# A two-layer attention and GLA trunk on one core: three stretches of instruction order rewritten

## The chip, the core and the metric

The kernel runs on one core of one Trainium2 chip. The core has engines with a queue each, and each queue is worked off in order: PE (TensorE) multiplies matrices, DVE (VectorE) and ACT (ScalarE) do elementwise work, POOL (GpSimd) does almost nothing here, and SP (SyncE) issues nearly all DMA transfers. Engines wait for one another through semaphores alone, so an instruction that waits holds up whatever stands behind it on its own engine. The metric is the time of one execution in microseconds (us), as the median of the runs.

## The reference

A decoder trunk of two layers over 1024 tokens of width 1024, in float32. Layer 0 mixes tokens with dilated sliding-window attention in three head groups, layer 1 with gated linear attention (GLA); each mixer is followed by a squared-ReLU MLP of width 4096.

```python
def reference(x, ...):
    for i in range(DEPTH):
        h = rmsnorm(x, norm_mix_w[i])
        if i % N_MIXERS == 0:
            x = x + dilated_attention(h, attn_w_in[j], attn_w_out[j])
        else:
            x = x + gla_mixer(h, gla_w_in[j], gla_w_gate_up[j], gla_b_gate[j], gla_norm_w[j], gla_w_out[j])
        h = rmsnorm(x, norm_mlp_w[i])
        x = x + sq_relu_mlp(h, mlp_w_up[i], mlp_w_down[i])
    return rmsnorm(x, final_norm_w)

def rmsnorm(x, w):
    return x * rsqrt(mean(x * x, axis=-1) + 1e-5) * w
```

What the change touches are three products with a norm beside them: the values of the attention, `h @ w_in` for three groups of 1024 columns; the values and the output gate of GLA, two further such products, of which the gate goes through silu; and the second half of the last MLP's `@ w_down` with the final `rmsnorm`.

## The kernel before

**Arithmetic.** Every matmul operand is cut into a rounded part (`hi`, fp32r) and the rest (`lo`): ACT copies the operand to fp32r, DVE subtracts that copy. One product then takes three matmuls, hi x hi, hi x lo and lo x hi (L213 to L215, L829, L1581). Large products are done by a seven-product scheme on 2x2 halves: the left operand's halves are `a11`, `a12`, `a21`, `a22` and four sums `s1` to `s4`, and seven products go into two accumulators, A and B, of four PSUM banks each, one bank for each block of 128 rows. There are eight banks in all.

**Values (L745 to L876).** `Values` computes one 1024x1024 product for each of three groups g. A group has 14 steps n = 14g + 2q + m: q is the product (operands in the order `ORDER`, L497: a12, a11, s1, s2, s4, s3, a22), m a half of the inner dimension. Each step has its weights loaded (`load`, SP), combined with those kept (`total`, DVE), rounded (`rounded`, ACT), their rest taken (`remain`, DVE; `prep` is the last three together), and multiplied (`product`, 24 matmuls of 128x512, six for each of four row blocks t). `sums` takes finished blocks out of PSUM: `copy` on ACT, `add` on DVE, then a store. Steps q = 0 go to B, q = 1 to A; their sum is the output block `c11`.

**The start (L1268 to L1373).** The first 1024 rows, x, come as four tiles of two row blocks. `Halves.norm` (L318, through L243 to L252) takes the squares of a pair on ACT, the inverse root over small ops on DVE and ACT, and scales with the norm weight `wbc` on DVE; `turn` transposes a pair on PE, four 128x128 into a bank, and ACT copies the bank out; `cut` makes hi and lo of 512 columns. Here the order of the work is written out by hand: pair 0, then steps 0 to 2 for row blocks 0 and 1, then pair 1, step 3, pair 2, and so on; `product(4)` (the first with `s1`) follows when all four pairs are turned. From step 8 a loop runs `sums`, `prep(n + 2)`, `load(n + 5)`, `product(n)`.

**GLA's values and gate (L878 to L929, L1729 to L1797).** `Mixed` is the same with 28 steps: g = 0 is the gate, g = 1 the values. The gate's blocks are kept in tiles `gq` of four blocks each from the pool `h8` (12 slots); silu is worked off one block for each step: `begin` (exp, ACT), `guard` (DVE), `logs` (two ACT passes), `close` (three DVE passes and a store to `ggscr`). In the loop over n, `W.pump()` (L161) issues the loads of the next weights and puts their rounding on ACT and DVE; it is called from n = 24 on. The pool `k4` (25 slots of 4 KB a partition) holds weights, their hi and lo, the sums' hi and lo, and the pair tiles; `t2` (8 slots) the small blocks.

**The end (L1646 to L1650, L1672 to L1703).** The last product ends in `run_end`: for each of the last four row blocks, 12 matmuls, `add` into x, then `half_out` (square on ACT, times the norm weight on DVE). After every second block the inverse root of both is taken in one chain (`rstd_of`, L225) and four halves are scaled and stored by SP, 256 KB each.

Of the kernel before, what the change touches and what calls it, by code (L numbers as in the profile page):

```python
# [41 lines left out]
def hybrid_trunk(ctx, tc, x, norm_mix, norm_mlp, norm_fin, a_in, a_out, g_in, g_up, g_b, g_nw,  # L42
# [702 lines left out]
    class Values:  # L745

        STEPS = 14 * NG
        small = False
        BLOCKS = ((1, 0), (0, 0), (0, 1), (1, 1), (1, 1), None, (1, 0))

# [100 lines left out]
        def sums(self, n):  # L851

            g, q, m = self.place(n)
            if q == 0 and g and m == 0:
                for t in range(4):
                    self.add("c21", "B", t, g - 1)
            for t in (2 * m, 2 * m + 1):
                if q == 1:
                    self.copy("c11", "B", t, g)
# [18 lines left out]
    class Mixed(Values):  # L878

        STEPS = 28  # L880
        small = True

        def __init__(self):
            super().__init__()
            self.quad, self.todo, self.open, self.last = {}, deque(), None, None

# [3 lines left out]
        def copy(self, name, s, t, g):  # L890
            if g:
                return super().copy(name, s, t, g)
            if t == 0:
                self.quad[name] = h8([P, 4, 512], F32, "gq")
            c = self.c[name, t] = self.quad[name][:, t, :]
            act.activation(c, self.acc[s][t], AF.Copy)
# [6 lines left out]

        def begin(self):

            if self.todo:
                d = t2([P, 512], F32, "gd")
                act.activation(d, self.todo[0][0], AF.Exp, scale=-1.0)
                self.open = [*self.todo.popleft(), d]

        def guard(self):
            if self.open is not None:
                dve.tensor_scalar(self.open[3], self.open[3], 1.0, 3e38, op0=OP.add, op1=OP.min)

        def logs(self):
            if self.open is not None:
                e = t2([P, 512], F32, "ge")
                act.activation(e, self.open[3], AF.Ln)
                act.activation(e, e, AF.Exp, scale=-1.0)
                self.last, self.open = [*self.open, e], None  # L920

        def close(self):
            if self.last is not None:
                c, rows, cols, d, e = self.last
# [3 lines left out]
                sp.dma_start(ggscr[rows, cols], c)  # L928
                self.last = None  # L929

# [336 lines left out]

    x0 = []  # L1268
    vals = Values()
    for p in range(NB // 2):  # L1270
        t = h8([P, 2, D], F32, "x0")
        for i in range(2):
            sp.dma_start(t[:, i, :], x[0, 256 * p + 128 * i:256 * p + 128 * i + 128, :])
        x0.append(t)
        if p == 0:
            wbc = load_norm_w(norm_mix[0])
            sp.dma_start(ident, ident_d)
            for n in range(4):
                vals.load(n)
    sp.dma_start(masks, msk)  # L1280
    hs = Halves(x0, wbc, vals, None)
    hs.norm(0, (512, 768, 0, 256), 256)
    vals.rounded(0)
    hs.turn(0, (2, 3))
    vals.remain(0)
    hs.cut("a12", 0)
    hs.turn(0, (0, 1))
    vals.prep(1)
    hs.cut("a11", 0)
    vals.prep(2)  # L1290
    vals.prep(3)
    hs.norm(1)
    for n in range(3):
        vals.product(n, [0, 1])
    hs.norm(2)
    hs.turn(1)
    vals.product(3, [0, 1])
    hs.cut("a12", 1)
    hs.cut("a11", 1)
    vals.load(4)  # L1300
    vals.load(5)
    hs.turn(2)
    hs.sum1(0)
    vals.total(4)
    hs.rstd(3)
    hs.norm(3)
    for n in range(2):
        vals.product(n, [2, 3])
    hs.cut("s1", 0)
    vals.rounded(4)  # L1310
    hs.turn(3)
    vals.remain(4)
    vals.product(2, [2, 3])
    vals.total(5)
    vals.sums(2)
    hs.sum1(1)
    hs.cut("s1", 1)
    vals.sums(3)
    vals.rounded(5)
    vals.product(3, [2, 3])  # L1320
    vals.remain(5)
# [7 lines left out]
    hs.cut("s2", 1)  # L1329
    vals.sums(4)  # L1330
    vals.sums(5)
    vals.remain(6)
# [5 lines left out]
    for c in range(2):  # L1338
        hs.cut("s4", c)
    hs.sum3()  # L1340
    vals.load(9)
    for n in range(6, 8):
        vals.sums(n)
        vals.load(n + 4)
        vals.product(n)
        vals.prep(n + 2)
        if n == 6:
            for c in range(2):
                hs.cut("s3", c)
        else:  # L1350
            for c in range(2):
                hs.cut("a22", c)
    vals.load(12)
    for n in range(8, vals.STEPS):
        if n == 12:
# [9 lines left out]
        if n == vals.STEPS - 1:  # L1365
            heads.stage(0, 2)
            heads.stage(0, 3)
        vals.sums(n)
        vals.prep(n + 2)
        vals.load(n + 5)  # L1370
        vals.product(n)
# [136 lines left out]
    class Down:  # L1508
# [117 lines left out]
        def hook(self, n):  # L1626
# [19 lines left out]
            elif n >= 52:  # L1646
                ss = sm([P, 2, 2], "ss")
                for t in (2 * (n - 52), 2 * (n - 52) + 1):
                    self.fin[t] = (ss, k4([P, D], F32, "fin"))
                    self.half_out(t, 1)  # L1650

# [19 lines left out]

        def half_out(self, t, n):  # L1672
            ss, o = self.fin[t]
            sl = slice(512 * n, 512 * n + 512)
            r = self.rows(4 + t)[:, sl]
            junk = t2([P, 512], F32, "junk")
            act.activation(junk, r, AF.Square, accum_out=ss[:, t % 2, n:n + 1])
            dve.tensor_tensor(o[:, sl], r, self.wbc[:, sl], op=OP.mult)

        def run_end(self):  # L1680

            for t in range(4):
                self.product(54, [t])
                self.product(55, [t])
                self.add("B", 1, t, 0)
                if self.spill is not None:
                    self.between(t)
                    continue
                self.half_out(t, 0)
                if t % 2 == 0:  # L1690
                    continue
                ss, _ = self.fin[t]
                v = sm([P, 2], "v")
                dve.tensor_tensor(v, ss[:, :, 0], ss[:, :, 1], op=OP.add)
                y = rstd_of(v, 2, 1.0 / D)
                for u in (t - 1, t):
                    _, o = self.fin.pop(u)
                    dst = out[0, 512 + 128 * u:640 + 128 * u, :]
                    k = u % 2
                    act.activation(o[:, :512], o[:, :512], AF.Copy, scale=y[:, k:k + 1])  # L1700
                    sp.dma_start(dst[:, :512], o[:, :512])
                    dve.tensor_scalar(o[:, 512:], o[:, 512:], y[:, k:k + 1], None, op0=OP.mult)
                    sp.dma_start(dst[:, 512:], o[:, 512:])  # L1703

# [24 lines left out]
    def gla_values():  # L1729
# [9 lines left out]
        m.load(5)  # L1739
        hs.sum1(0)  # L1740
        hs.cut("s1", 0)
        m.sums(2)
        m.product(2)
        m.prep(4)
        hs.sum1(1)
        hs.cut("s1", 1)
        m.load(6)
        m.sums(3)
        m.product(3)
        m.prep(5)  # L1750
        for c in range(2):
            hs.sum2(c)
        hs.cut("s2", 0)
        m.load(7)
        m.total(6)
        for n in range(4, m.STEPS):
            if n != 13:
                m.guard()
                m.close()
            if n != 5:  # L1760
                m.sums(n)
            if n == 4:
                m.sums(5)
                hs.cut("s2", 1)
            m.prep(n + 2)
            m.load(n + (4 if n < 5 else 5))
# [309 lines left out]
```

## Time and profile before

| what | us |
|---|---|
| median of 3 runs | 2612.7 (2612.32 to 2613.21) |
| the profiled execution, its time | 2613.06 |
| its span, first to last instruction | 2611.3 |
| ACT busy | 1276.7 (49%) |
| DVE busy | 1858.9 (71%) |
| PE weight loads (PEld) busy | 2157.3 (83%) |

The span lies inside the execution's own time; 1.8 us are around it. A busy PE isn't a PE at its peak: matmuls overlap, so one is shown with about 0.39 us although the next starts 0.23 us later. Lost PE time is therefore read from start times and counts. In rows of the timeline the first two numbers are start and length in us, xN is a count of merged instructions, and brackets give the engine's idle time ahead of the row and what ended it. Lnnn is a line of the kernel, SPq the queue that issues DMAs. On a row of groups, the numbers behind the bar are busy us in all and mean ns of one.

### The profile page before, as it was taken

The page shows a single profiled execution, that of the slowest core. Times are in us where ns is not written, and L with a number is a line of the kernel's source. Part 1 is how long each engine was busy: PE and PEld are TensorE (multiplying, and loading weights), DVE is VectorE, ACT ScalarE, POOL GpSimd, SP SyncE. Part 2 cuts the span into 40 slices and gives each one's busy share as a digit, 9 for nine tenths or more (in the row PEclk, how much of TensorE's full clock was granted, in tenths as well). Part 3 has the DMA queues.
Part 4 walks back from the last instruction along what each step waited for, and adds up shares of the span by engine and source line. Part 5 has one row for each costly group of instructions (what it writes and reads, how often), then busy time and mean ns, then how long its engine had stood idle before and what let it go on. Part 6 is the DMA issues. An engine that isn't in the chain of part 4 may idle for free.

```text
span 2611.3 us, 33042 instructions
## 1 busy us (share of the span) xinstructions
PE 2586.3 (99%) x12144; PEld 2157.3 (83%) x12144; DVE 1858.9 (71%) x2986; ACT 1276.7 (49%) x2319; POOL 1.8 (0%) x7
## 2 busy tenths in 40 slices
PE   8999999999999999999999999999999999999998
PEld 6888888888888888888888887878888888888887
DVE  7645888888888768666657577977658866666566
ACT  6332455555556446555533345654326545553343
POOL 0000000000000000000000000000000000000000
PEclk9999999999999999999999999999999999999999
DMA  5533465655556733454775452463513544396543
GB/s 190 169 129 124 103 161 131 163 147 150 155 151 183 227 121 128 167 169 137 283 252 185 137 194 93 133 199 97 187 66 123 170 153 157 131 355 200 189 146 125
DMA packets 327010, 423.12 MB, mean 162 GB/s; under 512 B 19808, under 2 KB 192224, under 8 KB 326848
## 3 DMA queue, kind: packets, MB, share of 16 engines
q1 hardware_dynamic: 326848, 421.01, 51.0%
q8 instruction: 95, 1.56, 0.3%
q14 instruction: 67, 0.55, 0.1%
HBM read 279.71 MB, written 116.06 MB: 152 GB/s over the span
## 4 chain that ended last, share of the span: by engine, by line
PE 87%; DVE 8%; ACT 3%; issue 1%; DMA 1%; SPq 0%; ACTq 0%; DVEq 0%
PE pX L598 16%; PE pB L1581 13%; PE pV L598 11%; PE pA L1581 10%; PE pY L598 5%; PE pZ L598 5%; PE pB L829 5%; PE pd L215 3%; PE pd L213 3%; PE pd L214 3%; PE pA L829 3%; PE pO L1017 2%; PE pS L976 2%; PE pP L1003 1%; DVE dl L814 1%
## 5 line engine op out<-in xcount | busy, mean ns | idle before, releaser
L1581 PE MATMUL pB<-dh 128*128 128x512 f32 x512 | 199.4, 389 | 0.0
L1581 PE MATMUL pB<-dh,dl 128*128 128x512 f32 x512 | 199.2, 389 | 0.0
L1581 PE MATMUL pB<-dl,dh 128*128 128x512 f32 x512 | 199.2, 389 | 0.0
L222 DVE TENSOR_TENSOR dl<-sin,dh 128x1024 fp32r<-128x1024 f32 x112 | 136.5, 1218 | 44.6 <-ACT dh L219 44.2
L219 ACT ACTIVATE dh<-sin 128x1024 fp32r<-128x1024 f32 x112 | 117.8, 1052 | 89.7 <-PE pB L1581 32.5
L219 ACT ACTIVATE dh<-kept 128x1024 fp32r<-128x1024 f32 x64 | 67.9, 1061 | 183.4 <-DVE kept L1546 137.8
L598 PE MATMUL pV<-s4h,wd 128*128 128x512 f32 x448 | 150.8, 398 | 0.0
L1581 PE MATMUL pA<-dh,dl 128*128 128x512 f32 x384 | 149.4, 389 | 0.0
L1581 PE MATMUL pA<-dl,dh 128*128 128x512 f32 x384 | 149.4, 389 | 0.0
L1581 PE MATMUL pA<-dh 128*128 128x512 f32 x384 | 149.4, 389 | 0.0
L992 ACT ACTIVATE pt<-pt,orow 128x128 f32<-128x128 f32 (+1 forms) x192 | 84.8, 443 | 96.7 <-DVE orow L990 94.6
L1581 PEld LDWEIGHTS pB<-dh,dl 128*128 128x128 f32 x512 | 96.1, 188 | 20.1
L1581 PEld LDWEIGHTS pB<-dh 128*128 128x128 f32 x512 | 96.1, 188 | 19.9
L1581 PEld LDWEIGHTS pB<-dl,dh 128*128 128x128 f32 x512 | 96.1, 188 | 19.8
L536 DVE TENSOR_TENSOR wal<-raw,wah 128x512 fp32r<-128x512 f32 x112 | 76.2, 686 | 42.9 <-ACT wah L535 42.9
L607 ACT ACTIVATE c<-c 128x512 f32<-128x512 f32 x64 | 40.4, 632 | 122.6 <-DVE c L635 78.9
L598 PEld LDWEIGHTS pV<-s4h,wd 128*128 128x128 f32 x448 | 84.2, 188 | 17.7 <-DVE rb L623 0.2
L222 DVE TENSOR_TENSOR dl<-kept,dh 128x1024 fp32r<-128x1024 f32 x64 | 78.3, 1224 | 25.1 <-ACT dh L219 19.3
L536 DVE TENSOR_TENSOR wbl<-t,wbh 128x1024 fp32r<-128x1024 f32 x56 | 68.6, 1225 | 38.3 <-ACT wbh L535 38.3
L990 DVE CUSTOM_DVE_ANT_0 pt<-pS,masks 128x128 f32<-128x128 f32 (+1 forms) x192 | 58.2, 347 | 51.2 <-PE pS L976 51.2
L598 PE MATMUL pY<-a12h,wah 128*128 128x512 f32 x224 | 89.5, 400 | 0.0
L598 PE MATMUL pZ<-a22h,wgh 128*128 128x512 f32 x224 | 89.3, 399 | 0.0
(336 smaller groups left out, 7364.2 us busy)
## 6 DMA issues: line engine op xcount, KB each, us to landing
sin<-acts SPq DMA_DIRECT2D x112, 512.0 KB, 3.8
raw<-in_mlp_w_up_dram SPq DMA_DIRECT2D x64, 512.0 KB, 6.0
acts<-s SPq DMA_DIRECT2D x64, 512.0 KB, 3.4
raw<-in_mlp_w_down_dram SPq DMA_DIRECT2D x64, 512.0 KB, 4.7
raw<-in_attn_w_in_dram SPq DMA_DIRECT2D x96, 256.0 KB, 4.6
cw<-c SPq DMA_DIRECT2D x192, 128.0 KB, 2.3
acts<-c SPq DMA_DIRECT2D x64, 256.0 KB, 2.1
kept<-in_mlp_w_down_dram SPq DMA_DIRECT2D x32, 512.0 KB, 5.8
```

The lines of the kernel that those rows point to most:

```text
L213: pe.matmul(ps, sh, mh, start=start, stop=False)
L214: pe.matmul(ps, sh, ml, start=False, stop=False)
L215: pe.matmul(ps, sl, mh, start=False, stop=stop)
L219: act.activation(hi, src, AF.Copy)
L222: dve.tensor_tensor(lo, src, hi.bitcast(F32), op=OP.subtract)
L536: self.remain(lambda: dve.tensor_tensor(lo, src, hi.bitcast(F32), op=OP.subtract))
L598: pe.matmul(st[b], u[:, k, :], v, start=first and k + n == 0, stop=k == 3 and n == 2, skip_group_check=True)
L829: pe.matmul(self.acc[s][t], a[:, c], b[:, k, :], start=fresh and m + k + v == 0, stop=m == 1 and k == 1 and v == 2, skip_group_check=True)
L976: pe.matmul(ps[:, i, :128 * n], self.qT[:, 128 * b:128 * b + 128], self.kT[:, k0:k0 + 128 * n], start=True, stop=True)
L990: dve.tensor_tensor_reduce(pt[:, i, :128 * n], ps[:, i, :128 * n], masks[:, m0:m0 + 128 * n], -scale, 1e38, op0=OP.add, op1=OP.min, accum_ ...
L992: act.activation(pt[:, i, :128 * n], pt[:, i, :128 * n], AF.Exp, scale=-1.0, bias=m, accum_out=self.row[:, r, HD:HD + 1])
L1581: pe.matmul(self.acc[s][t], a[:, k, c], b[:, k, :], start=fresh and m + k + v == 0, stop=m == 7 and k == 1 and v == 2, skip_group_check=True)
```

## The change

**Start.** The calls from L1268 to L1323 are replaced by a list at the grain of one block and one half of its columns. PE first runs 26 matmuls on a zeroed bf16 tile. x comes row block by row block, the first one and `wbc` in halves of 512 columns. For a block b: `sq`, `lne` and `nvz` give the inverse root, `xn` scales a half, `tr` transposes it (four transposes into one bank), `hi` and `lo` read that bank directly, and `ac` copies it into `a` later. Products go by one block (`pr(n, t)`, six matmuls). Steps 14 and 15 (group 1, q = 0) are loaded, rounded and multiplied here, between the last blocks, and left out of the loop (`ahead`, `plan`); their `c11` copies wait in two pair tiles of `k4`.

```diff
+        ahead = (1,)
...
-            if name == "c22":
+            if name == "c22" or (name == "c11" and g in self.ahead):
                 if t % 2 == 0:
-                    self.pair = k4([P, 2, 512], F32, "c22")
+                    self.pair = k4([P, 2, 512], F32, name)
...
+    warm = t2([P, 512], BF16, "warm")
+    pool.memset(warm, 0.0)
+    dve.memset(eps, EPS)
+    ps = bank("warm")
+    for _ in range(26):
+        pe.matmul(ps, warm[:, 0:P], warm, start=True, stop=True)
+    for c in (0, 512):
+        sp.dma_start(x0[0][:, 0, c:c + 512], x[0, 0:128, c:c + 512])
...
+    load_wbc(512)
+    sp.dma_start(ident, ident_d)
+    vals.load(0)
+    load_wbc(0)
+    vals.load(1)
+    load_rows(1)
+    vals.load(2)
+    vals.load(3)
+    load_rows(2, 3, 4, 5)
+    vals.load(14)
+    vals.load(15)
+    load_rows(6, 7)
...
+    def hi(b, half):
+        ps, h, l, a = spot(b, half)
+        act.activation(h, ps, AF.Copy)
+
+    def lo(b, half):
+        ps, h, l, a = spot(b, half)
+        dve.tensor_tensor(l, ps, h.bitcast(F32), op=OP.subtract)
+
+    def ac(b, half):
+        ps, h, l, a = spot(b, half)
+        act.activation(a, ps, AF.Copy)
...
+    nvz(0)
+    xn(0, 1)
+    rh(0)
+    tr(0, 1)
+    rl(0)
+    hi(0, 1)
+    lo(0, 1)
+    xn(0, 0)
+    rh(1)
+    pr(0, 0)
+    sq(1)
+    rl(1)
+    tr(0, 0)
+    lne(1)
+    hi(0, 0)
+    rh(2)
+    nvz(1)
+    xn(1, 1)
+    pr(1, 0)
+    lo(0, 0)
+    rl(2)
+    tr(1, 1)
+    hi(1, 1)
+    rh(3)
+    xn(1, 0)
+    pr(2, 0)
+    rl(3)
+    lo(1, 1)
+    sq(2)
+    lne(2)
+    tr(1, 0)
+    pr(3, 0)
...
+    rh(15)
+    pr(1, 3)
+    ad(1)
+    rl(15)
+    hs.xn[2] = [xn0.pop(4), xn0.pop(5)]
+    pr(2, 3)
+    hs.turn(2)
+    sq(7)
+    lne(7)
+    pr(3, 3)
+    nvz(7)
+    xn(7, 1)
+    xn(7, 0)
+    cp(3)
+    hs.sum1(0)
+    ad(2)
+    pr(14, 0)
+    hs.xn[3] = [xn0.pop(6), xn0.pop(7)]
+    pr(15, 0)
+    hs.turn(3)
...
-    for n in range(8, vals.STEPS):
+    plan = [n for n in range(8, vals.STEPS) if n // 14 not in vals.ahead or n % 14 > 1]
+    plan += range(vals.STEPS, vals.STEPS + 5)
+    for i, n in enumerate(plan[:-5]):
...
-        vals.prep(n + 2)
-        vals.load(n + 5)
+        vals.prep(plan[i + 2])
+        vals.load(plan[i + 5])
```

**GLA's stage.** `total` (DVE) moves ahead of the rounding of the same step, with other DVE work between; the gate's `c21` copies go to pairs in `k4` instead of a `gq` tile; the last `add` of `c12` comes a step earlier; two weight loads are issued at n = 23, and `W.pump()` starts at n = 25.

```diff
+            if name == "c21":
+                if t % 2 == 0:
+                    self.pair = k4([P, 2, 512], F32, "gp")
+                c = self.c[name, t] = self.pair[:, t % 2, :]
...
         hs.sum1(0)
+        m.total(4)
+        hs.sum1(1)
         hs.cut("s1", 0)
         m.sums(2)
         m.product(2)
-        m.prep(4)
-        hs.sum1(1)
+        m.rounded(4)
+        m.total(5)
+        m.remain(4)
         hs.cut("s1", 1)
         m.load(6)
         m.sums(3)
         m.product(3)
-        m.prep(5)
-        for c in range(2):
-            hs.sum2(c)
+        m.rounded(5)
+        hs.sum2(0)
+        m.remain(5)
+        hs.sum2(1)
...
-            if n != 5:
+            if n not in (5, 25):
                 m.sums(n)
...
+            if n == 24:
+                m.sums(25)
...
+            if n == 23:
+                W.dma()
+                W.dma()
...
-            if n >= 24:
+            if n >= 25:
                 W.pump()
```

**End.** Each block is finished by itself: its sum of squares is taken over 512, 256 and 256 columns, the first 512 ahead; one refining step follows the exp; the halves are scaled and stored while the next block is multiplied. The last block's first half is stored from ACT's queue.

```diff
+    def joined(self, t, c):
+        x = self.rows(4 + t)[:, c:c + 256]
+        dve.tensor_tensor(x, self.acc["B"][t][:, c:c + 256], x, op=OP.add)
...
+    def root(self, t):
+        ss, _ = self.fin[t]
+        dve.scalar_tensor_tensor(ss[:, 3:4], ss[:, 2:3], 1.0 / D, ss[:, 3:4], op0=OP.mult, op1=OP.add)
+        dve.tensor_scalar(ss[:, 4:5], ss[:, 3:4], -0.5, None, op0=OP.mult)
+        act.activation(ss[:, 5:6], ss[:, 0:1], AF.Ln, scale=1.0 / D, bias=ss[:, 3:4])
+        act.activation(ss[:, 6:7], ss[:, 5:6], AF.Exp, scale=-0.5)
+        self.weigh(t, 0, 256)
+        dve.scalar_tensor_tensor(ss[:, 4:5], ss[:, 0:1], -0.5 / D, ss[:, 4:5], op0=OP.mult, op1=OP.add)
+        self.weigh(t, 256, 256)
...
+            (act if last and not n else sp).dma_start(out[0, 512 + 128 * t:640 + 128 * t, c], o[:, c])
...
+                if t:
+                    self.polished(t - 1)
+                self.joined(t, 0)
+                if t:
+                    self.scaled(t - 1, 1)
+                self.square(t, 0, 256, 2)
+                self.joined(t, 256)
+                self.square(t, 256, 256, 0)
+                self.root(t)
+                if t:
+                    self.scaled(t - 1, 0)
+            if self.spill is None:
+                self.polished(3)
+                self.scaled(3, 1)
+                self.scaled(3, 0)
```

More of the change, by code (lines that the diff above doesn't have):

```diff
@@ L1265, in plan_merges @@
             at(t + 10, lambda half=half: join(half), 9)
-    x0 = []
+    x0 = [h8([P, 2, D], F32, "x0") for _ in range(NB // 2)]
     vals = Values()
[L1270 to L1279, printed above, removed]
+    eps = sm([P, 1], "eps")
@@ L1284, in hybrid_trunk @@
[L1284 to L1299, printed above, removed]
+    for name in ("a12", "a11"):
+        vals.h[name] = Split(hs.one(name + "h", F32R), hs.one(name + "l", F32R))
+    for half in range(2):
+        hs.a[0, half] = hs.one("a", F32)
@@ new lines, in xn, with tr, spot @@
+    def xn(b, half):
+        if b not in xn0:
+            xn0[b] = k4([P, D], F32, "xn")
+        sl = slice(512 * half, 512 * half + 512)
+        dve.scalar_tensor_tensor(xn0[b][:, sl], rows0(b)[:, sl], root0[b][:, 4:5], wbc[:, sl], op0=OP.mult, op1=OP.mult)
+    def tr(b, half):
+        ps = face[b, half] = bank("pT").rearrange("p (k t) -> p k t", k=4)
+        for k in range(4):
+            c = 512 * half + 128 * k
+            pe.transpose(ps[:, k, :], xn0[b][:, c:c + 128], ident)
+    def spot(b, half):
+        s, sl = vals.h[("a11", "a12")[half]], slice(128 * b, 128 * b + 128)
+        return face[b, half], s.hi[0][:, :, sl], s.lo[0][:, :, sl], hs.a[0, half][0][:, :, sl]
@@ new lines, in hi, with pr @@
+    def hi(b, half):
[7 more added lines that the diff above has]
+        act.activation(a, ps, AF.Copy)
+    def pr(n, *ts):
+        vals.product(n, list(ts))
+    rh, rl = vals.rounded, vals.remain
+    cp = lambda t, g=0: vals.copy("c11", "B", t, g)
+    ad = lambda t: vals.add("c11", "A", t, 0)
@@ new lines, in hybrid_trunk @@
+    pr(1, 1)
+    ac(0, 0)
+    sq(3)
+    lne(3)
+    cp(0)
+    tr(2, 1)
+    hi(2, 1)
+    pr(2, 1)
+    nvz(3)
+    xn(3, 1)
+    lo(2, 1)
+    tr(2, 0)
+    hi(2, 0)
+    xn(3, 0)
+    lo(2, 0)
+    ac(1, 1)
+    ac(1, 0)
+    pr(3, 1)
+    pr(0, 2)
+    sq(4)
+    lne(4)
+    ad(0)
+    cp(1)
+    tr(3, 1)
+    hi(3, 1)
+    pr(1, 2)
+    nvz(4)
+    xn(4, 1)
+    lo(3, 1)
+    tr(3, 0)
+    hi(3, 0)
+    xn(4, 0)
+    lo(3, 0)
+    pr(2, 2)
+    sq(5)
+    lne(5)
+    ac(2, 1)
+    ac(2, 0)
@@ L1367, in hybrid_trunk @@
             heads.stage(0, 3)
+        if n % 14 == 2 and n // 14 in vals.ahead:
+            for t in range(4):
+                vals.add("c21", "B", t, n // 14 - 1)
         vals.sums(n)
-        vals.prep(n + 2)
-        vals.load(n + 5)
+        vals.prep(plan[i + 2])
+        vals.load(plan[i + 5])
         vals.product(n)
```

177 lines of the change are left out of this document (115 added, 62 removed).

## The prediction

> **What bounds the kernel now.** I read the page's totals first, then the chain of waits, then counts of matmuls by stretch, and at last the timeline where the counts fall short.
>
> ```profile
> span 2611.3 us, 33042 instructions
> PE 2586.3 (99%) x12144; PEld 2157.3 (83%) x12144; DVE 1858.9 (71%) x2986; ACT 1276.7 (49%) x2319; POOL 1.8 (0%) x7
> PE   8999999999999999999999999999999999999998
> ```
>
> PE is busy 99% of the span; only the first and the last of the 40 slices (65 us each) fall to 8. A better order can't win more than PE's lost time, and that has to be looked for in the three stretches that the change touches. Two rows of the chain of waits give the unit:
>
> ```profile
> 89.19 21.76 PE pB L829 x96
> 67.36 10.95 PE pB L829 x47
> ```
>
> 96 matmuls take 21.76 us, 0.2267 us each, and from 67.36 us PE runs without a gap. How much is lost before that? Windows of the matmuls (L829) and of the transposes (L334) give the counts (the xN behind PE's busy time):
>
> ```profile
> 0.00:67.30 67.30, 45.46 (x193) 35.69 (x193) 1.00 0.52 184
> 0.00:44.50 44.50, 11.09 (x64) 8.47 (x64) 1.00 0.57 207
> ```
>
> 193 matmuls are 43.7 us; 64 transposes at 0.12 us (16 in 1.91, a row below) 7.6. 67.36 less these leaves **16.0 us lost at the start**. The same count for GLA's stage, and the largest wait of PE there:
>
> ```profile
> 1618.30:1643.40 25.10, 23.19 (x98) 17.73 (x97) 1.00 0.14 42
> 1665.10:1743.60 78.50, 77.14 (x339) 62.96 (x337) 1.00 0.53 161
> PE pB L829 <- DVE c L844: 1.2, 1, 1.2
> ```
>
> 98 matmuls are 22.2 of 25.1 us: 2.9 lost. 339 are 76.9 of 78.5: 1.6 lost, of which 1.2 is one wait for DVE. So **4.5 us in GLA's stage**. The end, by the timeline and the DMA view (last number: median us from issue to landing, here of the first of the last four stores and of the last two):
>
> ```profile
> 2601.89 0.39 PE L1581 MATMUL pB<-dh,dl 128*128 128x512 f32 x1
> 2602.31 0.69 DVE L1587 TENSOR_TENSOR xs<-pB,xs 128x512 f32<-128x512 f32 x1
> 2607.64 0.41 SPq L1703 DMA_DIRECT2D out_dram<-fin  x1
> out_dram<-fin SPq DMA_DIRECT2D x1, 256.0 KB, 2.1
> out_dram<-fin SPq DMA_DIRECT2D x2, 256.0 KB, 2.6
> ```
>
> The last matmul starts at 2601.9, the last store lands near 2607.64 + 2.6 = 2610.3, 1 us before the end: **8.0 us from the last add's start (2602.31) to the landing**. The change can win a part of 16.0 + 4.5 + 8.0 us, no more.
>
> **The change, part by part: the start.**
>
> ```profile
> 0.73 0.86 SPq L1273 DMA_DIRECT2D x<-in_x_dram  x2
> 2.59 1.00 SPq L771 DMA_DIRECT2D raw<-in_attn_w_in_dram  x2
> 4.50 1.06 ACT L243 ACTIVATE junk<-x 128x1024 bf16<-128x1024 f32 x1 [2.49 <-DMA x<-in_x_dram]
> raw<-in_attn_w_in_dram SPq DMA_DIRECT2D x1, 512.0 KB, 7.2
> 10.00:12.00 2.00, 2.00 (x11) 1.90 (x10) 2.00 (x6) 1.97 (x4) 0.00 (x0) 1.00 1.05 400
> 8.89 3.85 PE L334 MATMUL pT<-ident,xn 128*128 128x128 f32 x16 [8.89 <-DVE xn L252]
> 13.30 0.39 PE L829 MATMUL pB<-dl,a12h 128*128 128x512 f32 x1
> 14.22 0.50 PE L829 MATMUL pB<-dh,a12l 128*128 128x512 f32 x1 [0.53 <-DVE a12l L346]
> 28.04 1.91 PE L334 MATMUL pT<-ident,xn 128*128 128x128 f32 x16
> L1726 POOL MEMSET gc<- 128x512 f32 x1 | 0.5, 524 | 975.2 <-DVE wal L536 975.2
> 24.44 2.04 ACT L336 ACTIVATE a<-pT 128x512 f32<-128x512 f32 x4
> 25.35 2.74 DVE L252 SCALAR_TENSOR_TENSOR xn<-x,y,wbc 128x512 f32<-128x512 f32 x4
> 38.17 1.22 DVE L814 TENSOR_TENSOR dl<-kept,dh 128x1024 fp32r<-128x1024 f32 x1
> ```
>
> These are prices and three times: x's first block is there at 4.5 us, the first weights (issued at 2.6, 7.2 to landing) at 9.8, and the third matmul, the first that needs a12's rest, starts at 14.22. The DMA engines are full (share 1.05 at 400 GB/s, so 256 KB are 0.65 us).
>
> *The first matmul.* Half of the first block needs 256 KB: x is there at about 3.8 and 4.5. Two squares of half size, ln, exp and two small DVE ops end at 6.1; `xn` of 512 columns (2.74/4 = 0.69) at 6.8. The first weights stand behind 1.34 MB instead of 2.11: they land at about 7.5 (9.8 less 0.77 MB at 400 GB/s, less a little for the halved `wbc`), rounding (1.06) and rest (1.22) end at 9.85. The 26 warm-up matmuls come first on PE: a memset of 0.5 on POOL after the start at 0.7, so from about 1.2; POOL has nothing else to do. 16 transposes at 8.89 took 3.85, those at 28.04 only 1.91, and the matmul at 13.30 took the 0.39 of the last one at 2601.89: the clock rose about 4 us after PE's first work (by these lengths; the granted clock of the 10:12 row, the third number from its end, reads 1.00 throughout). A bf16 matmul of 512 columns is in no row; I take the fp32r step, 0.227, and twice that while the clock is low: 4.0/0.457 = 8.8 slow ones, 17.2 fast ones in 3.9, the end at **9.1**. (Bounds: all fast 7.1, all slow 13.0.) Four transposes to 9.6, `hi` on ACT to 10.35, `lo` on DVE to 11.05: the third matmul at 11.1, 3.1 earlier than 14.22.
>
> By the Trainium skill, "TensorE: Matmul & The Clock Gate", Part 4, transposes don't count as PE work for the clock gate; then the matmul at 13.30 would have run at half pace. The trace disagrees: only transposes ran ahead of them. Its Part 1 puts the slow time at one free-running window of 3.4 us, with 427 ns for a slow matmul of 512 columns; an estimate from this is 7.3 to 9.0 us for the 26, so an end between 8.5 and 10.2, and the sum would move by -0.6 to +1.1.
>
> *Block 0.* DVE now sets the pace: three more rests (1.22 each), three `xn` and a `lo` (0.69 each) and a root (three small ops, 0.55) are 7.0 us, a little less since each starts 0.08 before the one ahead has ended, a little more for ACT: the rest of step 3 is there at 17.7, and `pr(3, 0)`, five of its six matmuls behind it, ends at 18.9. PE has then done 24 matmuls (5.4) and 16 transposes (1.9): 11.5 lost.
>
> *From 18.9 on* PE has 12 + 8 groups of six and 48 transposes ahead, 33 us, and DVE about 30 us of work for them, ACT as much. For the first four blocks ACT does 16 half copies (`hi`, `ac`, 8.2 us) in place of 8 copies and 4 roundings of twice the size (8.3), so its sum is the old one; what costs is the order, since each engine's queue waits for the others'. Walking the three queues in order I find PE short at three places: `turn(2)` needs four banks while A holds four and B's last block one, and its copies stand behind `rh(15)` on ACT, so the fourth waits 1.3, and with it `pr(3, 3)` and all of PE behind it; `xn(7)` behind `lne(7)`: 0.2; `pr(0, 3)` for a bank that `ac(2, 1)` frees: 0.2. `product(4)` comes at 53 and needs `dl` of step 4 at 53: 0 to 0.6. So 13.4 lost against 16.0, a **gain of 2.6**. Steps 14 and 15 are the same matmuls earlier; they cover DVE's backlog, which now ends the gap ahead of 67.36. Bounds: +5.5 (no stall after block 0, warm-up at 8) and -3 (warm-up at 13, the stalls doubled).
>
> **GLA's stage.**
>
> ```profile
> 1601.82 1.23 DVE L814 TENSOR_TENSOR dl<-kept,dh 128x1024 fp32r<-128x1024 f32 x1 [1.13 <-ACT dh L808]
> 1607.90 1.23 DVE L814 TENSOR_TENSOR dl<-kept,dh 128x1024 fp32r<-128x1024 f32 x1 [1.13 <-ACT dh L808]
> 1624.54 1.22 DVE L814 TENSOR_TENSOR dl<-kept,dh 128x1024 fp32r<-128x1024 f32 x1 [1.19 <-ACT dh L808]
> 1631.30 1.23 DVE L814 TENSOR_TENSOR dl<-raw,dh 128x1024 fp32r<-128x1024 f32 x1 [0.86 <-ACT dh L808]
> 1659.89 0.34 SPq L928 DMA_DIRECT2D ggscr<-gq  x1
> 1662.18 1.09 ACT L896 ACTIVATE gq<-pA 128x512 f32<-128x512 f32 x2 [6.63 <-issue]
> 1726.00 0.31 ACT L151 ACTIVATE wboth<-raw 128x128 fp32r<-128x128 f32 x1 [4.38 <-DMA raw<-in_gla_w_in_dram]
> 1733.24 1.28 DVE L844 TENSOR_TENSOR c<-pB,c 128x512 f32<-128x512 f32 x2
> 1733.98 0.50 PE L829 MATMUL pB<-dh,a22h 128*128 128x512 f32 x1 [1.18 <-DVE c L844]
> ```
>
> DVE is what step 7 and step 8 wait for, and it stood idle four times for ACT's rounding of the very operand it had just combined. The new order puts a sum between at the first two: 1.13 + 1.13 = 2.26 us. Step 7's rest is then ready at 1623.5 instead of 1625.8, ahead of PE (1624.0): 1.7 gone. Step 8's at 1630.3, while PE would now ask at 1629.7: 0.6 of 1.2 stays. **2.3 won.** ACT's 6.63 us ahead of 1662.18 are put down to "issue"; what landed just before is the fourth block of `gq` for c11 (store issued at 1659.89, landing some 2.1 later), which frees the `h8` tile that c21's copies take. In pairs from `k4` they don't wait: 0.4, what is left of the 1.6. At 1726.00 ACT waits 4.4 for a load that `W.pump` issued just before, DVE behind it, and the last two adds of c12 (1733.24) behind DVE, which free the bank that PE waits for at 1733.98. With the add a step earlier, the loads at n = 23 and the pump at n = 25 this goes: **1.2**. On SP the two loads pass nothing but stores. Against it, `k4` holds two more tiles (c21) through ten steps; I charge 0.4. Sum **3.5**; bounds 4.5 and, short of the last rival, 0.
>
> **The end.**
>
> ```profile
> L1967 DVE TENSOR_TENSOR kdT<-pd,es 128x256 f32<-128x256 f32 x8 | 3.3, 417 | 0.0
> L1908 ACT ACTIVATE es<-ga 128x256 f32<-128x256 f32 x8 | 3.2, 404 | 0.0
> ```
>
> From the add at T = 2602.31: a half add 0.42 (next after 0.34), square 0.40 and read 0.19 twice on ACT, behind `scaled(2, 1)`, to T + 1.5; ln, exp to 1.95; DVE meanwhile weighs two quarters (0.42 each) and refines to 2.7; scaling 0.44 on DVE, 0.67 on ACT; the last stores are issued at T + 3.25 (SP) and 3.5 (ACT). Three stores of 256 KB follow `scaled(2, 0)` (issued 2.6): landings at 4.7, 5.35, 6.0, a DMA bound as before. T + 6.0 against T + 8.0: **2.0 won**. No row has a store from ACT's queue; I take SP's issue time. Bounds 1.0 and 2.6.
>
> **Sum.** 2.6 + 3.5 + 2.0 = 8.1: span 2603.2, the profiled execution 2613.06 - 8.1 = 2605.0, and since it stood 0.4 above the median of 2612.7, the forecast is **2604.6 us**.
>
> **Rivals.**
> *The start brings nothing* (chance 0.18): each bank is held by `ac` until late and ACT does 0.51 for each half more often; if every turn of the last four blocks stalls PE as `turn(2)` does, 2.6 is gone: 2607.2. For it: DVE and ACT have under 10% slack in my walk. Against: the first matmul is certainly earlier.
> *The warm-up outlasts the data* (0.10): the clock rises late and the 26 end at 13.0, 3.9 after my 9.1: 2608.5. The free-running window of the Trainium skill's page (as above) would give at most 2605.7.
> *The stage isn't reordered in effect* (0.10): DVE stays late, since its work for a step is what it was, or the slots of `k4` bind: 2604.6 + 3.5 = 2608.1. Against it: the idle rows above are waits, not work.
> *No stall after block 0* (0.15): the start wins 5.5: 2601.7.
> *Slower* (0.04): `k4`. 12 slots hold s2 to s4, 8 the rounded pairs of four steps, 6 or 7 kept and raw weights, 2 c22; c21 makes it 30 of 25. If rounding of step n + 2 has to wait until step n + 1 is multiplied, 1.06 + 1.22 us show in each of the ten steps while c21 is held: +23, so 2627 after the other gains. It decides once the shortage reaches from the pair just multiplied to the next one, four slots more than today's; c21 takes two, which speaks against it.
>
> **How the numbers follow.** Forecast 0.43, rivals as given. 0.2%, about what a measurement of this kernel can tell from no change, is 5.2 us: faster lies under 2607.5, slower over 2617.9. Forecast, the better case and most of the first rival lie under 2607.5: 0.79; the second and third and the rest of the first between: 0.16; slower 0.05. The range takes in both ends of the start less its far tail, and the mild rivals: 2600.5 to 2609.0.
>
> **What would show it.** Right: the third matmul of step 0 near 11 us; the row of `product(4)` near 53 with 48 more matmuls before it than today; no PE wait on `dl` of step 7, none for "DVE c L844" near 1730; last landing about 6 us after the last joined add. Wrong: warm-up matmuls past 10 us, PE waiting on ACT's `a` or `hi` after 20 us, ACT or DVE waiting for PE (slots) in steps 14 to 24 of GLA's stage, a store from ACT's queue that lands over 3 us after its issue.

## The result and the profile after

The changed kernel takes **2641.33 us** (median of 4 runs, 2640.79 to 2641.66), the kernel before on the same chip 2612.93 (4 runs): a ratio of 1.0108, 95% interval 1.0096 to 1.012. It is 28.4 us slower where 8.1 us faster was forecast.

The changed kernel's page, its first totals and PE's slices:

```profile
span 2639.9 us, 33180 instructions
PE 2628.7 (100%) x12170; PEld 2161.9 (82%) x12170; DVE 1863.9 (71%) x3014; ACT 1283.9 (49%) x2348; POOL 2.3 (0%) x8
PE   9999999999999999999999999999999999999998
```

PE's waiting did shrink. Before, 2586.3 of 2611.3 us were busy, 25.0 not; now 11.2 are not. But busy time itself grew by 42.4 us, of which the 26 warm-up matmuls are 8.1. The other 34 are no new work: the same matmuls got slower, as the rows below show. The chain of waits of the changed kernel (start, length, what) shows where:

```profile
67.42 11.20 PE pA L830 x48
...
2415.41 43.52 PE pB L1777 x192
```

48 matmuls of Values take 11.20 us, 0.2333 each; before, 96 took 21.76, 0.2267 each. 192 matmuls of Down take 43.52, still 0.2267. One group shows it without any scheduling; the view of single lines gives the count, the shortest, median and longest duration in ns. First the kernel before, then the changed one:

```profile
L598 PE MATMUL pX<-a11h,wah x224: 389/389/389, 252.2 to 2280.5; 128*128 128x512 f32 x112
...
L1581 PE MATMUL pB<-dh x512: 389/389/476, 1274.0 to 2601.4; 128*128 128x512 f32 x171
```

```profile
L598 PE MATMUL pX<-a11h,wah x224: 395/396/397, 257.6 to 2310.7; 128*128 128x512 f32 x112
...
L1777 PE MATMUL pB<-dh x512: 389/389/476, 1297.5 to 2632.2; 128*128 128x512 f32 x171
```

Not one of the 224 is at its old time; in Down nothing moved. The granted clock reads 1.00 for both in every window from 20 to 2600 us, so it isn't the clock. What tells the two groups apart is where their operands lie: `a11h` is an `h8` tile and `wah` a `k4` tile, while Down's `dh` and `dl` are both `k4`. The compiled programs give the places: a tag's slots are laid down when its first tile is allocated. Before, `h8` came first and `k4` next. The change allocates `eps` (tag `sm`) and `warm` (tag `t2`) ahead of `wbc`, the first `k4` tile, so 18,464 bytes of `sm` and `t2` slots now lie ahead of `k4`: its first slot moved from byte 101504 of each partition to 119968, while `h8` stayed at 3200. Modulo 256 the distance from `h8` to `k4` went from 0 to 32.

### The profile page after: what moved, and what is told of

The parts are those of the page before. It is cut to its first block, busy times and chain, and to the rows that moved or that the text cites. A ratio compares the mean times of both kernels' runs of the same rounds, so it can differ in the third digit from the quotient of the medians.

```text
span 2639.9 us, 33180 instructions
## 1 busy us (share of the span) xinstructions
PE 2628.7 (100%) x12170; PEld 2161.9 (82%) x12170; DVE 1863.9 (71%) x3014; ACT 1283.9 (49%) x2348; POOL 2.3 (0%) x8
## 4 chain that ended last, share of the span: by engine, by line
PE 98%; ACT 1%; DVE 0%; DMA 0%; issue 0%; SPq 0%; DVEq 0%
PE pX L598 18%; PE pB L1777 13%; PE pV L598 12%; PE pA L1777 10%; PE pB L830 8%; PE pA L830 6%; PE pZ L598 6%; PE pY L598 6%; PE pd L215 3%; PE pd L213 3%; PE pd L214 3%; PE pO L1026 2%; PE pS L985 2%; PE pP L1012 1%; PE pT L334 1%; PE pO L2075 1%
## 5 line engine op out<-in xcount | busy, mean ns | idle before, releaser
L603 ACT ACTIVATE e<-pX 128x512 f32<-128x512 f32 x96 | 56.5, 589 | 81.3 <-PE pX L598 81.3
```

Source lines behind the costliest of these rows:

```text
L603: act.activation(e, self.st[p]["X"], AF.Copy)
```

## The experiments

**1. The tags' places alone, put back and taken over.** Three kernels in which no instruction is added or left out. The first moves one allocation of the changed kernel up:

```diff
     vals = Values()
+    wbc, row = k4([P, D], F32, "wbc"), norm_mix[0]
     eps = sm([P, 1], "eps")
...
-    wbc, row = k4([P, D], F32, "wbc"), norm_mix[0]
```

> The changed kernel with one line moved: the first tile of tag k4 (wbc) is allocated ahead of eps and warm, so tag k4 starts at byte 101504 of a partition (a multiple of 128) as it did before, and not at 119968 (32 past a multiple of 64); no instruction is added or left out. Theory (the place of the tags sets the pace of the matmuls): start to start of the 512-column matmuls back from 233 to 227 ns everywhere, span about 2603, time 2604.6 us with 2601 to 2609 around it. Rival (the 26 warm-up matmuls and the clock that fell in the start leave TensorE slower): pace stays at 233 ns, 2641 us. Rival (the new order, its banks and its third queue slow TensorE): the same, 2641 us.

The second is the kernel before with the changed kernel's places:

```diff
         if p == 0:
+            sm([P, 1], "eps")
+            t2([P, 512], BF16, "warm")
             wbc = load_norm_w(norm_mix[0])
```

> The kernel before with two empty tiles, one of tag sm and one of tag t2, allocated between the first h8 tile and the first k4 tile: k4 starts at byte 119968, h8 stays at 3200; no instruction differs. Theory (place of the tags): 233 ns in Values, Up, Heads and out_proj where one operand is in h8 and the other in k4, 227 ns still in Down, whose operands are both in k4; time 2613 + 36 = 2649 us, 2644 to 2654. Rivals (warm-up, order of the start): 2613 us, 227 ns everywhere.

The third moves `h8` too:

```diff
+    eps = sm([P, 1], "eps")
+    warm = t2([P, 512], BF16, "warm")
     x0 = [h8([P, 2, D], F32, "x0") for _ in range(NB // 2)]
     vals = Values()
-    eps = sm([P, 1], "eps")
...
-    warm = t2([P, 512], BF16, "warm")
     pool.memset(warm, 0.0)
```

> The changed kernel with eps and warm allocated ahead of everything: h8 starts at 21664 and k4 at 119968, both 32 past a multiple of 64; no instruction differs. If it is the difference between the two operands' places that counts: 227 ns everywhere, 2604.6 us. If it is the place of k4 alone, or that any operand starts 32 past a multiple of 64: 233 ns, 2641 us or more (Down, with both operands there, would have to slow down too, but in the changed kernel it ran at 227 ns, which speaks against this). Warm-up or order: 2641 us.

Measured: 2605.88 us with `k4` allocated first (ratio to before 0.9971, 0.996 to 0.9981), 2647.27 for the kernel before with shifted places (1.013, 1.0112 to 1.0149), 2606.52 with both tags shifted (0.9974, 0.9963 to 0.9985). The chain of waits in the stretch of Values, one row each, in this order:

```profile
110.70 10.88 PE pA L830 x48
```

```profile
78.89 11.20 PE pA L829 x48
```

```profile
110.64 10.88 PE pA L830 x48
```

0.2267, 0.2333, 0.2267 us a matmul. Each of the three came out as the theory of places said and as no rival did. That settles the main question: no edit of the change costs the 28 us, the places alone do. The kernel before loses 33.8 us of span (2611.3 to 2645.1) by two empty tiles, and the changed kernel gets 35.2 back (2639.9 to 2604.7) by one moved line. It isn't the place of `k4` by itself either (the third kernel has it at 119968 as well): the distance between the two tags counts.

**2. Which distances are slow: matmuls alone.** All of the model is left out, and 96 matmuls a stage run with nothing beside them, with stationary and moving slices pushed on by a few bytes. `sa` and `mb` are `A` and `B`, except in the bf16 stages; s and m in a stage's name are the bytes of the push:

```diff
+    A = cst.tile([P, 2080], F32R, name="A")
+    B = cst.tile([P, 4128], F32R, name="B")
...
+            s = 128 * (i % 16) + so // size
+            m = cols * (i % (4096 // cols)) + mo // size
+            pe.matmul(ps[i // (n // 4)][:, 0:cols], sa[:, s:s + P], mb[:, m:m + cols], start=i % (n // 4) == 0,
...
+    for so in (0, 32, 64, 96):
+        for mo in (0, 32, 64, 96):
+            stage(f"s{so}m{mo}", [(so, mo)])
```

> All of the model is left out (out is x copied); what runs are stages of 96 matmuls, fp32r 128x128 by 512 columns, one name a stage: s is the byte at which the stationary operand starts past a multiple of 128, m the moving one's. Nothing else runs beside them. Theory (difference modulo 64 between the operands): 227 ns for s = m and for s and m 64 apart (s0m64, s32m96), about 233 ns for s0m32, s32m0, s0m96, s64m32 and the like. If it is each operand's own place: s32m32 slow as well. If it is the next weights' load that meets the running matmul's reads: stage own (pairs 0,0 and 32,32 by turns) slow and stage next (0,32 and 32,0 by turns) at 227. If it takes other engines' traffic beside the matmuls: 227 everywhere. Stages of 256 columns and of bf16 show whether it goes with the columns or with the instruction.

This missed: s0m0, which I held for the aligned stage, ran at 232.4 ns from start to start (the mean over the stage's 96 matmuls), s32m32 at 233.3, and the fastest were s4m0 (227.2), s96m32 (229.0) and s64m0 (229.1). The array `A` began at byte 5248 and `B` at 13568, 128 apart modulo 256: stage s0m0 had a distance of 128, not 0, and no stage had 0. But stages of one distance agreed within 1 ns (s0m32, s32m64, s64m96: 234.3, 234.3, 234.2), so the distance still ordered them, with some other modulus than 64. It needs no other engine's traffic. In bf16 all three stages ran at 216 ns, the median of the steps; their distances were 96, 128 and 160, so no bf16 stage had a distance of 0 to compare with.

Two kernels ask this of the whole model (the number of `sm` slots shifts `k4` by 96 bytes a slot), and a second set of stages has arrays that agree modulo 2048. With 20 slots:

```diff
-        return wk.tile(shape, F32, name=name, tag="sm", bufs=19)
+        return wk.tile(shape, F32, name=name, tag="sm", bufs=20)
```

> The changed kernel with tag sm given 20 slots instead of 19: k4 starts at byte 120064, a multiple of 128, 128 past the place of h8 when both are taken modulo 512; nothing else differs. Theory A (the operands' starts must agree modulo 64): 227 ns, 2605 us. Theory B, formed after the stages of matmuls alone, where 128 of difference ran at 232 to 233 ns though both were multiples of 64 (the starts must agree modulo 256 or 512): still 233 ns and 2641 us, with Down alone at 227.

With `bufs=24`:

> The changed kernel with tag sm given 24 slots instead of 19: k4 starts at byte 120448, which is 128 past a multiple of 512, as h8 at 3200 is; the order of the tags stays that of the changed kernel, and wbc is not moved. Theories A and B both: 227 ns everywhere, 2605.9 us as with k4 allocated first (2604 to 2608). If it were the order of the tags in memory, or sm and t2 lying between h8 and k4: 2641 us.

In the second set of stages `A` is longer, so that `B` begins 10,240 bytes, five times 2048, behind it, and the pushes go up to 480 bytes:

```diff
+STAGES = [(0, 0), (4, 0), (8, 0), (16, 0), (32, 0), (64, 0), (96, 0), (128, 0), (192, 0), (256, 0), (384, 0), (448, 0),
+          (480, 0), (0, 4), (0, 16), (0, 32), (0, 64), (0, 128), (0, 256), (32, 32), (64, 64), (16, 16), (128, 128)]
...
+    A = cst.tile([P, 2560], F32R, name="A")
+    B = cst.tile([P, 4608], F32R, name="B")
```

> The model is left out (out isn't computed); stages of 96 fp32r matmuls of 512 columns as before, now with the two arrays at starts that agree modulo 2048, so that stage s0m0 has a difference of 0. Theory B: 227 ns for s0m0, s32m32, s16m16, s64m64, s128m128, and 233 for differences of 16, 32, 64, 96; the stages with 128, 256, 384 tell the modulus (256: s256m0 at 227 and s128m0 at 233; 512: both at 233; 128: both at 227). Own (0,0 and 32,32 by turns) at 227 if a matmul's own two operands count, and next (0,32 and 32,0) at 233; the other way round if it is the next weights against the running columns. Fixed stationary or moving operands (sfix, mfix: difference 0; sfixo, mfixo: 32) 227 and 233 as well. If the difference is not what counts: no order in the stages.

With 20 slots (`k4` at 120064, a multiple of 128, distance 128): 2631.23 us (1.0068, 1.0047 to 1.0088). With 24 (120448, distance 0): 2605.96 (0.997, 0.9959 to 0.998). Their rows of the chain of waits:

```profile
111.69 11.15 PE pA L830 x48
...
2405.55 43.52 PE pB L1777 x192
```

```profile
112.26 10.88 PE pA L830 x48
```

A multiple of 64 is not enough, which ends theory A; the size under theory B was off (231 to 232 ns from start to start instead of 233, so 10 us less loss than I wrote). The stages, by groups of instructions (shape, count, busy us, mean duration in ns), slowest first:

```profile
L74 PE MATMUL s0m4x<-B,A 128*128 128x512 f32 x96 | 22.7, 396 | 0.0
...
L74 PE MATMUL ownx<-B,A 128*128 128x512 f32 x96 | 22.6, 396 | 0.0
...
L74 PE MATMUL s32m0x<-B,A 128*128 128x512 f32 x96 | 22.6, 395 | 0.0
...
L74 PE MATMUL s16m16x<-B,A 128*128 128x512 f32 x96 | 22.6, 396 | 0.0
...
L74 PE MATMUL sfixox<-B,A 128*128 128x512 f32 x96 | 22.6, 395 | 0.0
...
L74 PE MATMUL s128m0x<-B,A 128*128 128x512 f32 x96 | 22.5, 394 | 0.0
L74 PE MATMUL s0m16x<-B,A 128*128 128x512 f32 x96 | 22.4, 394 | 0.0
L74 PE MATMUL nextx<-B,A 128*128 128x512 f32 x96 | 22.4, 393 | 0.0
...
L74 PE MATMUL s0m64x<-B,A 128*128 128x512 f32 x96 | 22.1, 391 | 0.0
...
L74 PE MATMUL s32m32x<-B,A 128*128 128x512 f32 x96 | 22.0, 389 | 0.0
...
L74 PE MATMUL s0m256x<-B,A 128*128 128x512 f32 x96 | 21.9, 389 | 0.0
L74 PE MATMUL sfixx<-B,A 128*128 128x512 f32 x96 | 21.9, 389 | 0.0
...
L74 PE MATMUL s0m0x<-B,A 128*128 128x512 f32 x96 | 21.9, 389 | 0.0
L74 PE MATMUL s256m0x<-B,A 128*128 128x512 f32 x96 | 21.9, 389 | 0.0
```

21.9 to 22.0 us are 226.7 to 226.9 ns from start to start, 22.6 are 233 to 234. Fast are the distances 0 and 256 from starts that are multiples of 32; every other distance of this set is slow, from 228.9 (192) to 235.0 (the moving operand 4 bytes on). s16m16, which I expected at 227, is slow at distance 0, so the starts must be multiples of 32 as well (of those tried). It is the same with one fixed stationary slice (sfix, sfixo) and with one fixed moving slice (mfix 226.7, mfixo 233.3). Whether a matmul's own weights or the next one's count isn't settled: `own` and `next`, with places that change at every matmul, are both slow (233.7 and 231.6), and I had expected one of them at 227. With 256 columns it isn't there: 119.8 ns at distance 0, 118.3 at 32. The first set's s4m0 (distance 132, 227.2 ns) fits into no rule that I can give. Why the distance matters was not shown.

The Trainium skill, "TensorE: Matmul & The Clock Gate", Part 2 ("Step-by-step: what each phase is for"), says of the two operands that each has its own read port and that loading the next weights takes no bandwidth from the running matmul. No run here looks at ports; but a matmul whose cost depends on where its weights lie relative to its columns, 226.7 against 233.3 ns, is not what that sentence leads one to expect.

**3. The warm-up.** On the good places, without the memset and the 26 matmuls, which compute nothing of the output:

```diff
-    warm = t2([P, 512], BF16, "warm")
-    pool.memset(warm, 0.0)
...
-    ps = bank("warm")
-    for _ in range(26):
-        pe.matmul(ps, warm[:, 0:P], warm, start=True, stop=True)
```

> The changed kernel with k4 allocated first, and without the memset and the 26 warm-up matmuls. Theory (block 0 is paced by the landings of the second weights and of x's second block, not by TensorE): the third matmul of step 0 stays near 11.8 us or comes up to 0.4 earlier, the first 2 to 3 us of real matmuls run at half pace and that costs up to 1.5 us, of which later waits for DVE take up most; from 80 us on within 0.5 us of the kernel with warm-up, time 2606 (2605 to 2607.5). Rival (the warm-up is what wins the start): 2 to 3 us slower at 80 us, 2608.5. Rival (the warm-up outlasts the data and costs): 1 to 1.5 us faster at 80 us.

2605.41 us (0.9969, 0.9957 to 0.998), third matmul at 11.7 us, and 0.8 us ahead of the kernel with warm-up at 80 us, where I had allowed 0.5. Since traces of one kernel differ at the start, both were run again, and one with 12 warm-up matmuls (`range(12)`):

> The kernel without warm-up (k4 first) a second time, for its trace alone. Theory (a long warm-up followed by the sparse matmuls of block 0 lets the granted clock fall to half for 3 to 5 us between 11 and 18 us; without it that doesn't come): granted clock 1.00 in every stretch up to 22 us, first matmul of Heads near 251.2 us. Rival (the fall comes by chance in any kernel): a fall to 0.5 here too, Heads at 252 or later.

> The kernel with its 26 warm-up matmuls (k4 first) a second time, for its trace alone. So far three of five traces with the warm-up showed the clock at 0.5 for a time between 11 and 18 us. Theory: either it falls (Heads' first matmul at 252 to 253.6 us) or not (252.0); both later than 251.2 without warm-up.

> The kernel (k4 first) with 12 warm-up matmuls instead of 26: they end near 6.4 us, before the first normed half block (8.1), so that the transposes don't wait for them. Theory: transposes at 8.1 to 8.4 instead of 9.6; the clock is up or just about to rise, third matmul near 11.7; Heads' first matmul at 250.5 to 252. If the warm-up's length doesn't matter: 252.0.

Heads' first matmul, `pX`, is the first after all of Values. In the timelines of before, of `k4` first, and of the first and second kernel without warm-up:

```profile
252.22 0.39 PE L598 MATMUL pX<-a11h,wah 128*128 128x512 f32 x1
```

```profile
251.97 0.39 PE L598 MATMUL pX<-a11h,wah 128*128 128x512 f32 x1
```

```profile
251.16 0.39 PE L598 MATMUL pX<-a11h,wah 128*128 128x512 f32 x1
```

```profile
252.02 0.39 PE L598 MATMUL pX<-a11h,wah 128*128 128x512 f32 x1
```

The second trace of the kernel with warm-up had 251.66, both tags shifted 251.92, 24 `sm` slots 253.54, 12 warm-up matmuls 252.35 (their third matmul at 12.5, not 11.7). With 26 the row is thus at 251.7 to 253.5, without at 251.2 and 252.0: the warm-up buys nothing that shows. Besides the 0.8 at 80 us three expectations missed: the second trace without warm-up came 0.8 later than 251.2, the second with it earlier than the 252 I had put as its least, and the one with 12 matmuls later than its 250.5 to 252. Windows of PE (length, PE busy and count, granted clock, DMA share, GB/s) show what became of the clock. First three of the changed kernel, then one of `k4` first and one of the first kernel without warm-up:

```profile
6.10:12.92 6.82, 5.21 (x24) 1.00 1.00 374
12.92:16.33 3.41, 3.41 (x12) 0.50 1.05 409
14.00:16.00 2.00, 2.00 (x8) 0.50 1.05 414
```

```profile
14.00:16.00 2.00, 1.31 (x5) 1.00 1.05 413
```

```profile
14.00:16.00 2.00, 2.00 (x9) 1.00 1.04 409
```

In four of the six traces with 26 warm-up matmuls, and in the one with 12, the granted clock falls to 0.50 between 10.6 and 18 us: the clock that was bought is gone before block 0 is done. In the two that kept it, `k4` first and 20 slots, PE waited at most 0.85 us at a time between 9 and 19 us; in the four that lost it the longest wait, for `a12h` ahead of the first product, was 1.18 to 2.23 us. That is an order in six traces, not a cause shown. Nor does the fall decide the time: `k4` first kept its clock and came to Heads at 251.97, two that lost theirs at 251.66 and 251.92.

The 1.00 of the row without warm-up is no measurement. A trace lists the stretches of granted clock from the first rise on, and the view counts the time ahead of them as 1.00. The first stretch at 1.00 begins at 15.43 us in the first trace without warm-up, 16.10 in the second, 12.94 in the kernel before, and at 4.3 to 6.8 us with 26 warm-up matmuls. Ahead of these times matmuls start 0.43 us apart (the fp32r ones at 12.31 and 12.73 us of the first trace without warm-up, the bf16 ones of the warm-up), half pace. In all eleven traces of the model each stretch at one granted clock, but for the last one, at 0.50, which runs past the end of the work, lasts a whole multiple of 3.413 us (3.413 and 6.827 us at 0.50, for instance).

## Why the prediction was wrong, point by point

**The step that failed** is the first one: "Two rows of the chain of waits give the unit", 0.2267 us each, and the sentence ahead of it, "A better order can't win more than PE's lost time". Both take the time of a matmul as given and ask only what lies between matmuls. The unit was a property of the kernel before's places. Two allocations in the diff moved `k4` by 18,464 bytes, and the matmuls with one operand in `h8` and one in `k4` went from 0.2267 to about 0.2333 us: 33.8 us of span in the kernel before, where nothing else changed. My only slower rival did name `k4`, but the number of its slots (30 of 25), priced at +23 through rounding that waits; the changed kernel's waits of PE in GLA's stage list nothing at all. No term stood for places.

**The terms themselves** can be read on the kernel with `k4` first. GLA's stage runs from the first matmul on `a11h` to the first on `wboth`; the timelines of before and of `k4` first, the latter down to its last pair of half adds and its last store:

```profile
1596.51 0.47 PE L829 MATMUL pA<-dh,a11h 128*128 128x512 f32 x1
...
1743.67 0.39 PE L2010 MATMUL pd<-a11h,wboth 128*96 128x512 f32 x1
```

```profile
1596.94 0.48 PE L830 MATMUL pA<-dh,a11h 128*128 128x512 f32 x1
...
1739.26 0.39 PE L2248 MATMUL pd<-a11h,wboth 128*96 128x512 f32 x1
...
2597.90 0.75 DVE L1881 TENSOR_TENSOR xs<-pB,xs 128x256 f32<-128x256 f32 x2 [0.32 <-PE pB L1777]
...
2601.09 0.37 ACTq L1907 DMA_DIRECT2D out_dram<-fin  x1
```

The last number of its DMA view's row for that store is the time from issue to landing:

```profile
out_dram<-fin ACTq DMA_DIRECT2D x1, 256.0 KB, 2.8
```

| term | forecast | measured with `k4` first |
|---|---|---|
| start | -2.6 | -0.25 (252.22 to 251.97) |
| GLA's stage | -3.5 | -4.84 (147.16 to 142.32) |
| end, from the last adds to the landing | T + 6.0 | T + 6.0 (2597.90 to 2601.09 + 2.8) |
| whole | -8.1 | -7.4 by medians (-10.5 to -5.0); spans -6.6 |

With the places put back the sum is nearly right, but by luck: the start brought 2.35 us less than forecast, GLA's stage 1.34 more. Between these two stretches 0.7 us was lost (1344.29 us before, 1344.97 with `k4` first), for which no run gives a cause. The start's -0.25 is one trace's: on the good places Heads' first matmul came between 251.16 and 253.54 us, and never near the forecast's 249.6.

*Start: a size.* The third matmul of step 0 came at 11.8 with `k4` first (forecast 11.1), and the transposes behind the warm-up at 9.65 (forecast 9.1). What fell is "DVE now sets the pace" in block 0. ACT's timeline of `k4` first (idle before, and for what, in brackets):

```profile
8.82 1.06 ACT L809 ACTIVATE dh<-raw 128x1024 fp32r<-128x1024 f32 x1 [3.25 <-DMA raw<-in_attn_w_in_dram]
...
12.32 1.06 ACT L809 ACTIVATE dh<-raw 128x1024 fp32r<-128x1024 f32 x1 [1.44 <-DMA raw<-in_attn_w_in_dram]
13.60 1.06 ACT L1325 ACTIVATE junk<-x 128x1024 bf16<-128x1024 f32 x1 [0.22 <-DMA x<-in_x_dram]
```

The first weights land at 8.8, not 7.5, the second only at 12.3, x's second block at 13.6; ACT waits for all three, and DVE idles for ACT (2.8 us in two waits for `dh`). `pr(3, 0)` ends at 21.4, not 18.9: 2.5 of the 2.6 forecast. "The DMA engines are full" held for the kernel before's stretch from 10 us (share 1.05), not for the first 6 us here (share 0.60, 141 GB/s). The stalls after it were smaller than walked (`turn(2)` 0.4 instead of 1.3). `product(4)` came at 55.3 instead of 53. This is the rival *the start brings nothing* in its size, for another reason. By the Trainium skill, "TensorE: Matmul & The Clock Gate", Part 1, the estimate for the warm-up's end was 8.5 to 10.2; the traces agree, its row (start and length) ends at 8.5 to 9.8 in the six with 26. The forecast's reading that the clock rose about 4 us after PE's first work holds too: in the kernel before the first stretch at 1.00 begins at 12.94, 4.05 us after the first transpose, and only transposes had run by then. The 1.00 of its 10:12 row belongs to the time that the trace does not list. One reading of the count was off: the matmul behind the 16 transposes of 28.04 us starts 1.67 us after the first of them, so a transpose takes 0.104 us of PE's time, not 0.12, and the start had 16.9 us lost, not 16.0.

*GLA's stage: a size.* All that had been counted as lost was won. In the changed kernel and with `k4` first the waits of PE from 1596 us to the stage's end list nothing. The 0.6 that I left on step 8 went too, and the 0.4 charged for `k4` slots didn't come: 3.5 + 1.0 = 4.5, the upper bound I gave, against 4.84.

*End:* the time as worked out. The store from ACT's queue is issued at T + 3.2, 0.3 earlier than forecast, and lands 2.8 after its issue.

On the changed kernel's own places the same edits win less: 5.2 us of span (2645.1 to 2639.9). A slower PE waits less for the others to begin with: with the shifted places the kernel before has PE idle for 22.6 us (2645.1 less 2622.5 busy), not 25.0. How much of the difference that explains was not tested.

## What to carry to other kernels

A diff that allocates a tag's first tile earlier or later, or changes the size or number of any tag ahead of another, moves everything behind it: before pricing its instructions, compare the places of stationary and moving operands in both programs (here, for fp32r matmuls of 512 columns: distance a multiple of 256 bytes, starts multiples of 32). When busy time grows with the same instructions at the same granted clock, compare one group's duration, line by line, before looking at waits. And choose the place on purpose: the version with `k4` first keeps the change's gains and beats the kernel before by 0.3% (ratio 0.9971, 0.996 to 0.9981); that without warm-up (0.9969) can't be told from it.

## What the runs showed of the hardware that was not expected

- An fp32r matmul of 512 columns takes 226.7 ns from start to start when its operands' places differ by a multiple of 256 bytes in the partition (and are multiples of 32), and with one exception 229 to 240 otherwise (of the distances tried). With 256 columns (117 to 120) no such loss was seen. The three bf16 stages (216) agreed with one another, but none had a distance of 0.
- The effect needs nothing else running: stages of matmuls alone show it.
- The granted clock fell back to 0.50 after a warm-up that had raised it, between 11 and 18 us, in four of six traces with the 26 matmuls, while PE's longest wait there was 1.18 to 2.23 us; it lasted 3.41 us in three of them and 6.83 us in one.
- A granted clock of 1.00 ahead of a trace's first rise is not a measurement: there matmuls started 0.43 us apart. In the kernel before the clock rose at 12.94 us, when only transposes had run.
